# A two-layer encoder on one core: down's sum kept apart from the residual, the norm's factor of up moved behind it, and buffers placed anew

## The chip, the cores and the metric

The kernel runs on one core of a Trainium2 chip. The metric is the device time of one execution in microseconds (us), the median of several runs. The engines are called by the profile's names: PE is TensorE's matmul side and PEld its weight loads, DVE is VectorE, ACT is ScalarE, POOL is GpSimd, and SP is SyncE, whose queue issues all DMAs of this kernel.

## What is computed

A trunk of two layers over 1024 tokens of width 1024, in float32. Layer 0 mixes tokens by differential attention, layer 1 by neighbourhood attention on a grid. What follows the mixer is the same in both layers, and the change lies there:

```python
h = h + mix
h = h + swiglu(rmsnorm(h, norm_ffn[i]), ffn_w_gate[i], ffn_w_up[i], ffn_w_down[i])
gate = jax.nn.sigmoid(rmsnorm(h, norm_ple[i]) @ ple_w_gate[i])
h = h + gate * (p[i] @ ple_w_proj[i])
# swiglu(h, ...) = (silu(h @ w_gate) * (h @ w_up)) @ w_down, with 2816 hidden features
# rmsnorm(x, g) = x * rsqrt(mean(x * x) + eps) * g, per token
```

A norm over the last layer's output closes the trunk.

## The kernel before

Activations lie transposed: features on the 128 partitions, the 1024 tokens along the free dimension, in two halves f1 and f2 of 512. For precision every operand of a product is split in a high part (a cast, line 103 on ScalarE or 105 on GpSimd) and a low part (the difference, line 106 on VectorE), and every product is three matmuls (`PASSES`).

The feed-forward products use a Strassen scheme of seven products in place of eight. `blocks` (line 207) makes the seven weight operands from the raw weights: GpSimd forms the sums and differences (line 227), `split` casts them. `seven` (line 244) runs the products in the order 0, 5, 4, 1, 6, 3, 2 and calls `after` behind each, which takes an accumulator out of PSUM and combines it.

`out_proj` (line 634) adds the mixer's output to the residual x, writes x to memory (`hd`), and `moving_blocks` (line 146) makes the seven token operands `bt` from x times the norm's weights. It also adds up the squares of x (lines 672, 673). The norm's per-token factor, `rb`, is not applied there. `inverse_rms` forms it after the second product of the first group.

`gate_up` (line 677) has 11 pairs of hidden feature blocks. Each has a gate group and an up group of 84 matmuls (line 707). For gate, the sum is multiplied by `rb` (714), passed through silu (715), and multiplied by `rb` again on GpSimd (716), so that the up sum, multiplied in at line 718, needs no factor of its own. `hand_over` (746) makes down's seven operands of each pair, and they go to memory (`ad`), except the last pair's, which are kept.

`down` (line 790) goes over the pairs in five chunks (four of two pairs, one of three), and in each over four pairs of output blocks, `dp` and `dp + 4`. The operands come back from memory (`b`, line 787). Eight tiles `h` of 128 x 1024 are loaded from `hd` before (line 937), and every chunk's sums are added to them (line 828, some on VectorE from PSUM, some on GpSimd from a temporary).

`ple_proj` (line 853) and `ple` (883) end the layer: the norm (line 118) sums squares (123, 125), brings the factor to all partitions by two small matmuls (128, 136), and multiplies (139) into tiles `n`. The last norm's `n` go straight to the output (903).

Buffers: raw weights have two (`stage`), weight operands three slabs of 8 KB per partition and two more in the stage's own pool, and four buffers of 4 KB in `t4` hold temporaries, among them the weights' sums `s` and the products' `t`. Pools on the left are stacked in the order in which they are opened, so a pool that is opened after another was closed lies on the same memory, and a tile waits for the last access of the tile that lay there. In layer 0 the pool of x (four tiles of 8 KB, then 4 KB of sums of squares, 4 KB of squares and 8 KB of `n`) is followed on the same memory by the pools of the odd heads' q and k (24 KB), of v (24 KB) and of the even heads' q and k (24 KB).

The order of the instructions within each engine's queue is not the program's: a planner sets it at compile time, with a simulated timeline in which earlier program order goes first among what is ready. On the chip each queue is run in that order.

## Time and profile before

| | us |
|---|---|
| median of 3 runs | 3092.09 |
| lowest, highest | 3088.83, 3095.67 |
| the profiled execution's own time | 3095.93 |
| its span, first to last instruction | 3094.1 |

The page gives the busy time of each engine, the span in 40 slices, and the costliest groups of instructions. A group's row ends with the time that its engine sat idle ahead of it and what ended most of that. In a timeline a row has its start, its length, engine, line, operation, what it writes and reads, how many instructions were merged, and in brackets the idle time before it and what ended that. A wait for several things is put down to the one that came last.

### The profile page before, as it was taken

The numbers are of one execution on the slowest core, as the hardware profiler recorded it, in microseconds if no ns is written. First come the engines' busy times: TensorE is split into PE (matmuls) and PEld (weight loads), VectorE is DVE, ScalarE is ACT, GpSimd is POOL, SyncE is SP. The second block draws the span as 40 slices with busy tenths as digits, with TensorE's granted clock in tenths as the row PEclk, the third lists the DMA queues.
The fourth block names the chain that finished last, engine by engine and source line by source line (L and its number), as shares of the span: only waits on it lengthen the run. The fifth ranks groups of instructions, "written<-read, shape, count | busy, mean of one in ns | idle before, by whom it ended". The sixth has DMA issues, their size and how long they took to land. (4 is left out here: it accounts for less than half of the span.)

```text
span 3094.1 us, 38448 instructions
## 1 busy us (share of the span) xinstructions
PE 2820.4 (91%) x13272; PEld 2281.7 (74%) x13272; DVE 2277.1 (74%) x4023; ACT 1250.2 (40%) x2626; POOL 1572.7 (51%) x1408
## 2 busy tenths in 40 slices
PE   4999999997899999888899999999799999888888
PEld 4778778885677777666678888888577777666666
DVE  6697878787687787767576666666788877766666
ACT  3354546445343343222333544544434434322241
POOL 1234343435677777556422443333677777656522
PEclk8999999998899999999999999999899999999989
DMA  2101010324243333744232111135233333664222
GB/s 97 41 28 42 28 41 26 137 102 165 89 150 134 131 143 130 305 160 180 94 100 85 53 67 73 63 149 215 86 143 141 145 141 132 240 229 156 96 75 102
DMA packets 102291, 364.93 MB, mean 118 GB/s; under 512 B 11728, under 2 KB 13904, under 8 KB 98000
## 3 DMA queue, kind: packets, MB, share of 16 engines
q1 hardware_dynamic: 102096, 362.47, 32.2%
q8 instruction: 105, 1.72, 0.2%
q14 instruction: 90, 0.74, 0.1%
HBM read 249.18 MB, written 113.25 MB: 117 GB/s over the span
## 5 line engine op out<-in xcount | busy, mean ns | idle before, releaser
L707 PE MATMUL mm<-bt,w 128*128 128x512 f32 x3696 | 895.2, 404 | 51.0 <-ACT t L723 29.4
L707 PEld LDWEIGHTS mm<-bt,w 128*128 128x128 f32 x3696 | 707.3, 192 | 239.5 <-ACT t L723 38.5
L822 PE MATMUL mm<-b,w 128*128 128x512 f32 x1680 | 440.1, 416 | 76.8 <-ACT w L103 29.9
L106 DVE TENSOR_TENSOR w<-raw,w 128x512 fp32r<-128x512 f32 (+2 forms) x460 | 379.6, 845 | 129.3 <-ACT w L103 128.2
L822 PEld LDWEIGHTS mm<-b,w 128*128 128x128 f32 x1680 | 326.0, 198 | 184.9 <-ACT w L103 42.0
L103 ACT CAST w<-raw 128x512 fp32r<-128x512 f32 (+2 forms) x460 | 217.9, 498 | 479.3 <-DMA raw<-gu 170.3
L261 PE MATMUL d<-hnT,w 128*128 128x512 f32 x1536 | 386.2, 400 | 0.0
L261 PEld LDWEIGHTS d<-hnT,w 128*128 128x128 f32 x1536 | 287.2, 189 | 64.1
L105 POOL TENSOR_SCALAR w<-st 128x1024 fp32r<-128x1024 f32 (+3 forms) x128 | 146.5, 1146 | 360.3 <-PE mm L261 66.4
L828 POOL TENSOR_TENSOR h<-h,t 128x512 f32<-128x512 f32 x120 | 161.4, 1359 | 229.1 <-DVE t L828 196.3
L348 PE MATMUL d<-w,hnT 128*128 128x256 f32 x1536 | 227.8, 293 | 12.6 <-DVE v L106 7.8
L348 PEld LDWEIGHTS d<-w,hnT 128*128 128x128 f32 x1536 | 210.6, 196 | 23.6 <-DVE v L106 9.4
L106 DVE TENSOR_TENSOR w<-s,w 128x512 fp32r<-128x512 f32 (+2 forms) x184 | 194.8, 1064 | 26.4 <-ACT w L103 23.2
L106 DVE TENSOR_TENSOR w<-st,w 128x1024 fp32r<-128x1024 f32 (+3 forms) x128 | 142.6, 1118 | 91.6 <-POOL w L105 91.4
L421 ACT ACTIVATE e<-e,mx 128x1024 f32<-128x1024 f32 x128 | 147.4, 1152 | 133.7 <-DVE mx L419 125.8
L261 PE MATMUL mm<-hnT,w 128*128 128x512 f32 x768 | 189.3, 407 | 4.8 <-ACT hnT L103 3.3
L436 POOL TENSOR_SCALAR e<-e,rc 128x1024 f32<-128x1024 f32 x64 | 74.2, 1159 | 216.9 <-DVE rc L434 199.8
L261 PEld LDWEIGHTS mm<-hnT,w 128*128 128x128 f32 x768 | 147.7, 193 | 46.4 <-issue 8.3
L103 ACT CAST at<-tr 128x512 fp32r<-128x512 f32 (+2 forms) x288 | 131.8, 480 | 108.3 <-PE tr L571 69.5
L106 DVE TENSOR_TENSOR at<-tr,at 128x512 fp32r<-128x512 f32 (+2 forms) x288 | 155.8, 550 | 26.6 <-ACT at L103 19.9
L333 PE MATMUL s<-kh,qs 128*128 128x512 f32 (+2 forms) x384 | 154.1, 410 | 22.0 <-DVE mx L413 12.7
L567 POOL TENSOR_SCALAR e<-e,sm 128x384 f32<-128x384 f32 (+1 forms) x128 | 75.3, 590 | 184.3 <-DVE sm L566 158.3
(164 smaller groups left out, 5059.7 us busy)
## 6 DMA issues: line engine op xcount, KB each, us to landing
ad<-put SPq DMA_DIRECT2D x140, 512.0 KB, 2.7
b<-ad SPq DMA_DIRECT2D x140, 512.0 KB, 7.3
raw<-gu SPq DMA_DIRECT2D x88, 512.0 KB, 4.4
raw<-wd SPq DMA_DIRECT2D x40, 512.0 KB, 3.9
st<-wpg SPq DMA_DIRECT2D x32, 512.0 KB, 3.5
ot<-ot SPq DMA_DIRECT2D x14, 1024.0 KB, 3.9
o<-ot SPq DMA_DIRECT2D x14, 1024.0 KB, 8.4
st<-da_qk SPq DMA_DIRECT2D x16, 512.0 KB, 3.5
```

The costliest lines, as they stand in the source:

```text
L103: hi_engine.copy(out=w[0], in_=src)
L105: hi_engine.tensor_scalar(out=w[0], in0=src, scalar1=1.0, scalar2=0.0, op0=ALU.mult, op1=ALU.add)
L106: self.nc.vector.tensor_tensor(out=w[1], in0=src, in1=w[0].bitcast(F32), op=ALU.subtract)
L261: self.nc.tensor.matmul(ps, w[:, i, kt * P:(kt + 1) * P], self.hnT[half][:, j, kt, :], start=kt == 0 and n == 0, stop=kt == KT - 1 and n == 2)
L333: self.nc.tensor.matmul(s, qs[:, m, qc], (kh, kl)[part][:, m, kc], start=part == 0, stop=part == 1)
L348: self.nc.tensor.matmul(ps, self.hnT[t // 4][:, i, k, c], ws[k // 4][:, j, (k % 4) * 256:(k % 4 + 1) * 256], start=k == 0 and n == 0, stop ...
L421: nc.scalar.activation(out=e[m], in_=e[m], func=AF.Exp, bias=mx[:, m:m + 1], scale=SLOPES[h], accum_out=sm[:, m:m + 1])
L436: nc.gpsimd.tensor_scalar(out=e[0], in0=e[0], scalar1=rc[:, 0:1], scalar2=0.0, op0=ALU.mult, op1=ALU.add)
L567: nc.gpsimd.tensor_scalar(out=e[:, :n], in0=e[:, :n], scalar1=sm, scalar2=0.0, op0=ALU.mult, op1=ALU.add)
L707: self.end = nc.tensor.matmul(acc, w[b][:, i, k * P:(k + 1) * P], bt[b][:, j, k], start=first and k == 0 and n == 0, stop=k == 3 and n == ...
L822: nc.tensor.matmul(acc, w[b][:, i, q * P:(q + 1) * P], mv[b, q][:, j], start=first and q == 0 and m == 0, stop=q == n - 1 and m == 2, skip ...
L828: eng.tensor_tensor(out=o, in0=x, in1=y, op=ALU.add)
```

## The change

- `norm` has two `n` buffers in place of four. In `ple` the pool of the norm's tiles is opened on the right side.
- In `out_proj` the squares and the two differences of `moving_blocks` share one tag with two buffers in place of one buffer each.
- In layer 0's attention the pools are opened as odd, even, v.
- The weights' sums in `blocks` get a pool of their own with one buffer. In `down` the third temporary u3 is a half-size tile.
- `gate_up` no longer multiplies silu's output by `rb`. `rb` moves to a pool on the right that lives through `down`.
- `down` no longer loads the residual ahead. The first chunk writes its sums into `h` (copies by ScalarE where they were additions on VectorE). After the last chunk of each output pair the residual is loaded into `x`, `h` is multiplied by `rb` on GpSimd and x is added on VectorE.

```diff
 def norm
-            n = pool.tile([P, HALF], F32, tag="n", name="n", bufs=4)
+            n = pool.tile([P, HALF], F32, tag="n", name="n", bufs=2)
 def moving_blocks
-        t2 = pool.tile([P, HALF], F32, tag="t2", name="t2", bufs=1)
-        t3 = pool.tile([P, HALF], F32, tag="t3", name="t3", bufs=1)
+        t2 = pool.tile([P, HALF], F32, tag="t", name="t2", bufs=2)
+        t3 = pool.tile([P, HALF], F32, tag="t", name="t3", bufs=2)
 def out_proj
-                    sq = op.tile([P, HALF], F32, tag="sq", name="sq", bufs=1)
+                    sq = op.tile([P, HALF], F32, tag="t", name="sq", bufs=2)
 def blocks
-        sums = self.t4.tile([P, 2, HALF], F32, tag="t4", name="s")
+        sums = pool.tile([P, 2, room], F32, tag="s", name="s", bufs=1)
 def diff_attention
-            odd, vp, even = pool("da_qk1", 1), pool("da_v", 1), pool("da_qk0", 1)
+            odd, even, vp = pool("da_qk1", 1), pool("da_qk0", 1), pool("da_v", 1)
 def gate_up
-            pp, gp, sp, tp = pool("gput"), pool("ggt"), pool("gslab"), pool("gtmp")
+            ws, pp, gp, sp, tp = pool("gsum"), pool("gput"), pool("ggt"), pool("gslab"), pool("gtmp")
-            rb = tp.tile([P, S], F32, tag="rb", name="rb")
+            rb = self.rb
                         nc.scalar.activation(out=o, in_=o, func=AF.Silu)
-                        nc.gpsimd.tensor_tensor(out=o, in0=o, in1=rb[:, c], op=ALU.mult)
 def down
-                    w = self.blocks(parts, place)
+                    w = self.blocks(parts, place, sp, 3 * P)
+                    begin = chunk is CHUNKS[0]
...
                         elif b == 5:
-                            add(t["u2"], acc, t["p1"])
-                            add(lo[:, f2], lo[:, f2], t["u2"], nc.gpsimd)
+                            u2 = lo[:, f2] if begin else t["u2"]
+                            nc.vector.tensor_tensor(out=u2, in0=acc, in1=t["p1"], op=ALU.add)
+                            if not begin:
+                                gather(lo[:, f2], u2, nc.gpsimd)
                         elif b == 4:
-                            add(hi[:, f2], hi[:, f2], acc)
+                            if begin:
+                                nc.scalar.copy(out=hi[:, f2], in_=acc)
+                            else:
+                                gather(hi[:, f2], acc)
...
                         elif b == 6:
-                            add(t["u3"], acc, t["p1"])
-                            add(hi[:, f2], hi[:, f2], t["u3"], nc.gpsimd)
-                            add(hi[:, f1], hi[:, f1], t["u3"], nc.gpsimd)
+                            u3 = hi[:, f1] if begin else t["u3"]
+                            nc.vector.tensor_tensor(out=u3, in0=acc, in1=t["p1"], op=ALU.add)
+                            gather(hi[:, f2], u3, nc.gpsimd)
+                            if not begin:
+                                gather(hi[:, f1], u3, nc.gpsimd)
...
                     self.seven(banks, product, after)
+
+                    if chunk is CHUNKS[-1]:
+                        for dt in (dp, dp + 4):
+                            x = sp.tile([P, S], F32, tag="x", name="x", bufs=2)
+                            nc.sync.dma_start(out=x, in_=self.hd[dt])
+                            for c in (f1, f2):
+                                nc.gpsimd.tensor_tensor(out=h[dt][:, c], in0=h[dt][:, c], in1=self.rb[:, c], op=ALU.mult)
+                                nc.vector.tensor_tensor(out=h[dt][:, c], in0=h[dt][:, c], in1=x[:, c], op=ALU.add)
 def build
+                rp = tc.alloc_tile_pool(name=f"rb{layer}", bufs=1, side="right", reuse_waits="tile")
+                self.rb = rp.tile([P, S], F32, tag="rb", name="rb")
...
-                h = {t: hp.tile([P, S], F32, tag=f"h{t}", name=f"h{t}") for t in (0, 4, 1, 3, 7, 5, 2, 6)}
-                for dt in (0, 4, 1, 5, 2, 6, 3, 7):
-                    nc.sync.dma_start(out=h[dt], in_=self.hd[dt])
+                h = {t: hp.tile([P, S], F32, tag=f"h{t}", name=f"h{t}") for t in (0, 4, 1, 5, 3, 7, 2, 6)}
...
+                rp.release()
                 self.open_hn()
-                self.ple(layer, h, ps, pool("n"), proj)
+                np = tc.alloc_tile_pool(name=f"n{layer}", bufs=1, side="right", reuse_waits="tile")
+                self.ple(layer, h, ps, np, proj)
+                np.release()
```

## Rows read from the trace of the kernel before

**Rows 1.** The page, busy time of each engine and digits of the slices.

```profile
PE 2820.4 (91%) x13272; PEld 2281.7 (74%) x13272; DVE 2277.1 (74%) x4023; ACT 1250.2 (40%) x2626; POOL 1572.7 (51%) x1408
...
PE   4999999997899999888899999999799999888888
```

**Rows 2.** Groups by line: busy us, mean ns, idle before, its end.

```profile
L707 PE MATMUL mm<-bt,w 128*128 128x512 f32 x3696 | 895.2, 404 | 51.0 <-ACT t L723 29.4 <-DVE bt L106 10.4 <-DVE w L106 5.8
...
L822 PE MATMUL mm<-b,w 128*128 128x512 f32 x1680 | 440.1, 416 | 76.8 <-ACT w L103 29.9 <-ACT t L831 27.8 <-DMA b<-ad 11.9
...
L828 POOL TENSOR_TENSOR h<-h,t 128x512 f32<-128x512 f32 x120 | 161.4, 1359 | 229.1 <-DVE t L828 196.3 <-DMA h<-hd 29.1 <-ACT w L103 3.7
...
L716 POOL TENSOR_TENSOR gt<-gt,rb 128x512 f32<-128x512 f32 x88 | 129.9, 1495 | 25.6 <-ACT gt L715 25.6
...
L828 DVE TENSOR_TENSOR h<-h,mm 128x512 f32<-128x512 f32 x160 | 105.4, 678 | 45.6 <-POOL h L828 30.7 <-PE mm L822 11.6 <-DMA h<-hd 2.8
...
L106 DVE TENSOR_TENSOR v<-d,v 128x128 fp32r<-128x128 f32 x128 | 35.2, 284 | 31.6 <-ACT v L103 30.9
```

**Rows 3.** Timelines of the start: start, duration, operation, its wait and releaser.

```profile
59.18 1.42 DVE L106 TENSOR_TENSOR hnT<-n,hnT 128x256 fp32r<-128x256 f32 x4
...
61.01 1.48 ACT L103 CAST v<-d 128x128 fp32r<-128x128 f32 x8
...
62.45 13.69 PE L348 MATMUL d<-w,hnT 128*128 128x256 f32 x96 [7.78 <-DVE v L106]
75.97 22.64 PE L261 MATMUL d<-hnT,w 128*128 128x512 f32 x96
```

**Rows 4.** The tile of the sums, 1000 to 1240 us: groups by line.

```profile
L106 DVE TENSOR_TENSOR w<-s,w x24: 630/1561/1785, 1008.9 to 1231.5; 128x512 fp32r<-128x512 f32 x22, 128x256 fp32r<-128x256 f32 x2
...
L227 POOL TENSOR_TENSOR s<-s,raw x12: 745/1622/1630, 1006.8 to 1230.3; 128x512 f32<-128x512 f32 x11, 128x256 f32<-128x256 f32 x1
```

**Rows 5.** Timeline of one steady gate/up pair, layer 0.

```profile
1054.57 1.30 POOL L227 TENSOR_TENSOR raw<-raw,s 128x512 f32<-128x512 f32 x1 [1.30 <-DVE w L106]
...
1060.00 0.62 ACT L103 CAST w<-raw 128x512 fp32r<-128x512 f32 x1 [3.48 <-DMA raw<-gu]
...
1061.23 4.21 POOL L716 TENSOR_TENSOR gt<-gt,rb 128x512 f32<-128x512 f32 x3 [1.96 <-ACT gt L715]
...
1063.10 0.63 ACT L715 ACTIVATE gt<-gt 128x512 f32<-128x512 f32 x1 [1.42 <-DVE gt L714]
...
1064.25 39.61 PE L707 MATMUL mm<-bt,w 128*128 128x512 f32 x168 [2.16 <-ACT t L723]
...
1065.40 1.75 POOL L227 TENSOR_TENSOR s<-raw 128x512 f32<-128x512 f32 x1
```

**Rows 6.** Timelines of the begin of down, layer 0.

```profile
1257.21 9.28 SPq L937 DMA_DIRECT2D h<-hd  x8
...
1267.59 1.29 POOL L828 TENSOR_TENSOR h<-h,t 128x512 f32<-128x512 f32 x1 [14.99 <-DMA h<-hd]
...
1299.62 12.90 PE L822 MATMUL mm<-b,w 128*128 128x512 f32 x42 [3.63 <-ACT w L103]
```

**Rows 7.** Timeline of the last chunk of down, layer 0.

```profile
1482.37 2.71 POOL L828 TENSOR_TENSOR h<-h,t 128x512 f32<-128x512 f32 x2 [2.42 <-DVE t L828]
...
1486.43 2.13 PE L822 MATMUL mm<-b,w 128*128 128x512 f32 x8 [1.59 <-ACT w L103]
...
1495.41 1.29 POOL L828 TENSOR_TENSOR h<-h,t 128x512 f32<-128x512 f32 x1 [6.55 <-DVE t L828]
```

**Rows 8.** The same timeline, from the last output pair on.

```profile
1520.53 18.65 PE L878 MATMUL mm<-w 128*128 128x512 f32 x81 [1.44 <-POOL w L105]
...
1539.70 0.63 ACT L123 ACTIVATE acc<-h 128x512 f32<-128x512 f32 x1
```

**Rows 9.** Timeline of the end of the program.

```profile
3084.81 2.72 DVE L139 SCALAR_TENSOR_TENSOR n<-h,g,bc 128x512 f32<-128x512 f32 x4 [2.23 <-PE bc L136]
3087.70 2.81 DVE L139 SCALAR_TENSOR_TENSOR n<-h,g,bc 128x512 f32<-128x512 f32 x4 [0.17 <-DMA out<-n]
```

More of the change, by code (lines that the diff above doesn't have):

```diff
@@ L203, in packed, with blocks @@
         return place
-    def blocks(self, parts, place):
+    def blocks(self, parts, place, pool, room=HALF):
         nc = self.nc
@@ L694, in prepare @@
                     gates[pr] = gp.tile([P, 2, S], F32, tag="gt", name="gt", bufs=2)
-                return self.blocks([(raw[0][:, f1], raw[0][:, f2], raw[1][:, f1], raw[1][:, f2])], place)
+                return self.blocks([(raw[0][:, f1], raw[0][:, f2], raw[1][:, f1], raw[1][:, f2])], place, ws)
             def group(pr, which):
@@ L813, in down @@
                         parts.append((r[:, :, 0, 0], r[:, :, 1, 0], r[:, :, 0, 1], r[:, :, 1, 1]))
-                    w = self.blocks(parts, place)
+                    w = self.blocks(parts, place, sp, 3 * P)
                     banks = [ps.tile([P, HALF], F32, tag="mm", name="mm") for _ in range(4)]
-                    a2, b2 = (self.t4.tile([P, 2, HALF], F32, tag="t4", name="t") for _ in range(2))
-                    t = {"p1": a2[:, 0], "u2": a2[:, 1], "u3": b2[:, 0]}
+                    begin = chunk is CHUNKS[0]
+                    a2 = self.t4.tile([P, 2, HALF], F32, tag="t4", name="t")
+                    t = {"p1": a2[:, 0], "u2": a2[:, 1]}
+                    if not begin:
+                        t["u3"] = self.t4.tile([P, HALF], F32, tag="t4", name="t")
                     def product(b, acc, first):
@@ L824, in product, with gather @@
                                                  skip_group_check=True)
+                    lo, hi = h[dp], h[dp + 4]
+                    def gather(o, x, eng=nc.vector):
+                        eng.tensor_tensor(out=o, in0=o, in1=x, op=ALU.add)
                     def after(b, acc):
-                        def add(o, x, y, eng=nc.vector):
-                            eng.tensor_tensor(out=o, in0=x, in1=y, op=ALU.add)
-                        lo, hi = h[dp], h[dp + 4]
                         if b == 0:
@@ L837, in after @@
                         elif b == 1:
-                            add(lo[:, f1], lo[:, f1], acc)
+                            if begin:
+                                nc.scalar.copy(out=lo[:, f1], in_=acc)
+                            else:
+                                gather(lo[:, f1], acc)
                         elif b == 6:
-                            add(t["u3"], acc, t["p1"])
-                            add(hi[:, f2], hi[:, f2], t["u3"], nc.gpsimd)
-                            add(hi[:, f1], hi[:, f1], t["u3"], nc.gpsimd)
+                            u3 = hi[:, f1] if begin else t["u3"]
@@ L843, in after @@
+                            nc.vector.tensor_tensor(out=u3, in0=acc, in1=t["p1"], op=ALU.add)
+                            gather(hi[:, f2], u3, nc.gpsimd)
+                            if not begin:
+                                gather(hi[:, f1], u3, nc.gpsimd)
                         elif b == 3:
-                            add(hi[:, f1], hi[:, f1], acc)
+                            gather(hi[:, f1], acc)
                         elif b == 2:
-                            add(lo[:, f2], lo[:, f2], acc)
+                            gather(lo[:, f2], acc)
```

## The prediction

> **What bounds the kernel now.** I read the page first, for who is busy, then the groups by line, for what TensorE waits on, then the timelines of the four places that the change touches. On the page TensorE is busy 2820 us of 3094 and no other engine comes near it [rows 1]; its products are not changed. So the question is only which of its idle stretches go or come, and everything else counts as far as it ends one of them. The groups by line give those stretches in the two stages that are touched most: TensorE sat idle 51.0 us ahead of the gate/up products, 29.4 of them until the copy at L723, and 76.8 us ahead of down's products, 29.9 until a weight cast and 27.8 until the copy at L831 [rows 2]. Each total is for both layers. The copies are short; the reader is to see in the timelines what stands ahead of them in their queue. The first slice of the page, where TensorE is busy four tenths, is the third place.
>
> **The change part by part, each with its cost.**
>
> *Start.* The change swaps the pool of v with the pool of the even heads. By the pools' sizes in the code (x takes 32 KB, its squares and norms 16; q/k of the odd heads take 24 KB and v the next 24), v lies over the last quarter of x, the squares and n, so no v can be written before the last norm has read them. The timeline shows that: the first eight v casts run at 61.01, just behind the last hnT piece (59.18 + 1.42 = 60.6), though their products were long done, and TensorE, out of accumulators, idles 7.78 us and runs 96 value products from 62.45 to 75.97 [rows 3]. With v on free memory half of these, of the third quarter, can run while the fourth is normalised, and 48 x 13.69 / 96 = 6.8 us of work are left behind 60.6, partly overlapped with its last pieces. The end of the values moves from 76 to 64 at best: 12 us. Against this stand the v pieces on VectorE that now come before the last norm: 12 of 0.28 us [rows 2], 3.4 us on an engine that paces this stretch. I take -9, ends -4 and -12. Two n buffers in place of four make VectorE wait for a cast in the last quarter: +1, ends 0 and +3.
>
> *Moving blocks and first gate group.* Squares and the two differences share two buffers in place of three. Squares get double buffering, but a block's differences wait for the squares of the block before. TensorE's idle time ahead of the gate/up products outside the L723 wait is 51.0 - 29.4 = 21.6 us, 10.4 of it on these bt pieces [rows 2]. I take -2, ends -6 and +4, a modest share of either sign since both edits meet here.
>
> *Steady gate/up pairs.* The change drops 88 GpSimd products of 1.50 us, 130 us in all, from GpSimd's queue [rows 2]. What they hold up: in the pair shown, raw weights have landed by 1060.00, but the weights' first sum starts at 1065.40, straight behind three of these products (4.21 us from 1061.23). ScalarE waits 3.48 us for raw weights, which could only be loaded when the sums before had freed their buffer; then its queue holds the silu that waits on VectorE, and only then the copy that TensorE waits 2.16 us for [rows 5]. With sums some 4 us earlier the load, the cast and the copy come earlier by up to as much, more than the 2.16 us. TensorE's products set the bound: the gain cannot pass 29.4. Cover that goes: none, since silu's output is read later by VectorE and GpSimd, and a factor less only brings that forward. I take -20, nearer the upper end because the measured delay is twice the stall, ends 0 and -29. What is late next: the raw loads, behind two stage buffers.
>
> *Sums in a buffer of their own.* One buffer means that the next group's sum waits for the last reader of this one's: GpSimd's last subtraction of the up group ends at 1055.87, the next sum at 1065.40 is 9.5 us later [rows 5], so this wait is free. Four temporaries are left to the products' own tiles.
>
> *Begin of down.* Eight residual loads leave the SP queue, where they took 9.28 us of issue behind the b loads, and GpSimd no longer sits 14.99 us on them. Two GpSimd additions of 1.36 us per output pair go, 16 in all; two VectorE additions of 0.68 become ScalarE copies [rows 2, 6]. The queue freed here holds the weights' sums; in the trace TensorE's 3.63 us wait on a weight cast at 1299.62 follows [rows 6]. The b loads stay and with them TensorE's first waits. I take -5 for both layers, ends 0 and -9.
>
> *Middle of down.* Only the sums' buffer changes. GpSimd's order (product additions between the sums) stays in the code. I take -4, ends -20 (a third of the 57.7 us on casts and copies in [rows 2]) and +6, three stalls of 2 us if the compile-time order comes out worse.
>
> *End of down.* New: 16 GpSimd products by rb per layer, 32 in all, priced as the nearest row, L828's 1.36 us: 43.5 us; as many VectorE additions of 0.68; eight residual loads per layer on the SP queue, with two buffers, so a load waits for an addition and the next weight loads wait behind it. In a group of the last chunk GpSimd idles 2.42 and 6.55 us, more than 4 x 1.36 = 5.4, but a product of three of the four quarters is ready when the additions of 2.71 us end, and what comes next in that queue is the sum whose cast TensorE already waits 1.59 us for [rows 7]. The last pair's products meet the splits that TensorE waits 1.44 us for at L878; behind those the norm's squares wait in ScalarE's queue until 1539.70 anyway [rows 8]. Ends 0 (all in the idle 6.55) and +43.5 (all ahead of the sums). I take +14, a third: one and a third products of the four per pair.
>
> *Norms.* The very end: eight n in four buffers start at 3084.81, the fifth waits 0.17 for a landing at 3087.70 [rows 9], so a buffer turns round in 2.9 us. In two buffers four rounds follow each other: the starts are 84.8, 87.7, 90.6, 93.5, the last n ends at 94.9 in place of 90.5: +4, ends +3 and +5. The inner norms: +1, ends 0 and +3.
>
> The sum: -9 + 1 - 2 - 20 - 5 - 4 + 14 + 4 + 1 = **-20 us**. The profiled execution took 3095.93 (span 3094.1), 3.84 above the median of the runs shown; 3092.09 - 20 = **3072 us**.
>
> **A rule against it.** The VectorE difference that makes a weight's low part from two SBUF operands has a median of 1.56 us and reaches 1.79, while GpSimd's sums run beside it with a median of 1.62 [rows 4]; an addition with one operand in PSUM takes 0.68 [rows 2]. The Trainium skill, SBUF — State Buffer, section "Who interferes with whom", says why: a VectorE instruction with two SBUF inputs and a GpSimd instruction that reads SBUF exclude each other for a whole instruction. By that rule the new products by rb, beside new additions of two SBUF inputs, could each block one; by the row that is 1.56 - 0.68 = 0.9 us, 32 x 0.9 = 29 us more on VectorE, and the sum would be +9 if all of it reached TensorE. It gives back as much in gate/up, where 88 go.
>
> **Rivals.**
> - *More comes free* (0.21): the start at -12, gate/up at -29, the begin at -9, the middle at -20, the first group at -6, the end as taken with the norms: -12 - 29 - 9 - 20 - 6 + 20 = -56, 3036 us. For it: one GpSimd queue stands behind most of the stalls. Against: the raw loads and their two buffers stay.
> - *GpSimd's products were hidden* (0.13): then steady gate/up and middle give 0, the sum is +4, 3096 us. For it: the copy's wait ends on ScalarE behind a DMA, not on GpSimd directly.
> - *The products by rb go ahead of the weights' sums* (0.14), slower: the full 43.5 in the last chunk in place of 14, the sum is +9.5, 3102 us. It decides from 34 us on, 4.2 us per output pair. For it: they come before the next weights in program order, and are ready. Against: 6.55 us idle.
> - *The buffer does not free the sums, and the order made anew at compile time adds a stall per pair* (0.05): steady +29 in place of -20: +29, 3121 us. Against: 9.5 us of room.
>
> **How the numbers follow.** The forecast has 0.47, with 3050 to 3086 as its own range. Measurement can tell about 0.2%, 6.2 us. Faster: 0.47 + 0.21 = 0.68; within: 0.13; slower: 0.14 + 0.05 = 0.19. The range 3036 to 3102 leaves out the last rival and a third of the first and the third, whose prices are points with bounds on both sides: 0.05 + 0.07 + 0.05 = 0.17.
>
> **What would show it.** Right: v casts near 25 and values done near 66; L716 gone and GpSimd busy some 100 us less; the L723 wait below 10 us; no GpSimd wait on residual loads at the begin of down; the last n some 4 us later. Wrong: L723's wait unchanged, or TensorE's waits on weight casts in the last chunk above 4 us each.

## The result, and the profile after

The changed kernel takes 2965.18 us (median of 4 runs, 2963.36 to 2966.93) against 3093.88 of the kernel before in the same runs: a ratio of 0.9582, 95% interval 0.9561 to 0.9604. That is 129 us less, where 20 were forecast, and 71 us below the range's lower end. The direction was right and the size was not.

The page after, the rows that answer to [rows 1]:

```profile
PE 2768.3 (93%) x13272; PEld 2259.2 (76%) x13272; DVE 2255.2 (76%) x4039; ACT 1253.9 (42%) x2642; POOL 1451.2 (49%) x1336
...
PE   7999999997899999899799999999799999899987
```

TensorE is busy 52 us less for the same 13272 matmuls and idle 77 us less. The groups after, to be read against [rows 2] (down's products are on L824 now, the additions to h on L831):

```profile
L707 PE MATMUL mm<-bt,w 128*128 128x512 f32 x3696 | 886.5, 401 | 43.5 <-ACT bt L103 14.9 <-DVE bt L106 10.6 <-ACT t L722 10.6
...
L824 PE MATMUL mm<-b,w 128*128 128x512 f32 x1680 | 411.9, 401 | 34.3 <-ACT w L103 19.3 <-DVE t L838 9.6 <-DVE w L106 3.6
...
L831 POOL TENSOR_TENSOR h<-h,t 128x512 f32<-128x512 f32 x96 | 134.2, 1412 | 55.9 <-DVE t L853 41.9 <-DVE t L838 13.6
...
L831 DVE TENSOR_TENSOR h<-h,mm 128x512 f32<-128x512 f32 x144 | 95.3, 676 | 32.1 <-PE mm L824 22.4 <-POOL h L831 9.6
...
L869 POOL TENSOR_TENSOR h<-h,rb 128x512 f32<-128x512 f32 x32 | 46.1, 1447 | 10.1 <-DVE h L831 10.1
...
L870 DVE TENSOR_TENSOR h<-h,x 128x512 f32<-128x512 f32 x32 | 34.0, 1073 | 5.6 <-POOL h L869 5.6
```

Idle time ahead of gate/up's products went from 51.0 to 43.5 us, but ahead of down's from 76.8 to 34.3, and a down product lasts 401 ns in the mean where it lasted 416. The last two rows are the new work at the end of down.

Where the 129 us lie is worked out from the starts of TensorE's products in the two timelines, from the first product of a stage to the first of the next, both layers added:

| stretch | before | after | difference | forecast |
|---|---|---|---|---|
| start and attention, layer 0 | 710.3 | 690.9 | -19.4 | -9 +1 |
| out_proj and gate/up, to the last gate/up product | 1051.2 | 1018.8 | -32.5 | -2 -20 |
| from there to down's second chunk | 106.3 | 109.6 | +3.3 | -5 |
| second to fourth chunk | 306.7 | 236.2 | -70.6 | -4 |
| last chunk | 138.7 | 133.6 | -5.1 | +14 |
| ple_proj and ple | 273.6 | 269.5 | -4.2 | +1, with the next row |
| attention, layer 1 | 488.5 | 483.2 | -5.3 | |
| behind the last product | 18.9 | 23.4 | +4.5 | +4 |

More than half is the middle of down, the part that was thought least of. TensorE in that stretch of layer 0, and in the second 40 us of the program, as a table of windows (stretch, length, busy time and matmuls, granted clock, DMA share, GB/s), first the kernel before:

```profile
core 0: us, PE busy (x), PEclk, DMA share, GB/s
40.00:80.00 40.00, 20.65 (x125) 0.70 0.04 14
1293.00:1446.00 153.00, 131.20 (x506) 0.93 0.51 187
```

and after:

```profile
40.00:80.00 40.00, 37.69 (x205) 1.00 0.12 40
1258.00:1376.00 118.00, 118.00 (x505) 1.00 0.63 240
```

In the kernel before 153 us held 131.2 of busy time at a mean clock of 0.93 of full speed; after, the same products fill their 118 us without a gap at 1.00. So of the 35 us lost there, 21.8 were idle time and 13.2 were products that ran slowly. The row 40 to 80 answers the start: 37.7 us busy at clock 1.00, where the kernel before had 20.65 at 0.70.

The start itself, the timeline that answers to [rows 3]:

```profile
31.54 0.27 ACT L103 CAST v<-d 128x128 fp32r<-128x128 f32 x1 [0.17 <-PE d L348]
...
55.73 2.03 PE L261 MATMUL d<-hnT,w 128*128 128x512 f32 x8
57.60 4.47 PE L348 MATMUL d<-w,hnT 128*128 128x256 f32 x36
61.91 17.95 PE L261 MATMUL d<-hnT,w 128*128 128x512 f32 x76
```

The first v cast is at 31.5 in place of 61.0, from there on no wait ahead of the value products is longer than 0.8 us, their last run begins at 57.60, and products of the next stage are already done between them. And the end, the rows that answer to [rows 9]: n in pairs, each pair waiting 1.5 us for its buffers to be written out.

```profile
2951.69 1.41 DVE L139 SCALAR_TENSOR_TENSOR n<-h,g,bc 128x512 f32<-128x512 f32 x2 [2.23 <-PE bc L136]
...
2954.60 1.41 DVE L139 SCALAR_TENSOR_TENSOR n<-h,g,bc 128x512 f32<-128x512 f32 x2 [1.50 <-DMA out<-n]
2957.51 1.41 DVE L139 SCALAR_TENSOR_TENSOR n<-h,g,bc 128x512 f32<-128x512 f32 x2 [1.51 <-DMA out<-n]
2960.41 1.41 DVE L139 SCALAR_TENSOR_TENSOR n<-h,g,bc 128x512 f32<-128x512 f32 x2 [1.50 <-DMA out<-n]
```

### The profile page after: what moved, and what is told of

Same layout as the page of the kernel before. It is cut to its first block, busy times and chain, and to the rows that moved or that the text cites. A ratio compares the mean times of both kernels' runs of the same rounds, so it can differ in the third digit from the quotient of the medians.

```text
span 2964.9 us, 38407 instructions
## 1 busy us (share of the span) xinstructions
PE 2768.3 (93%) x13272; PEld 2259.2 (76%) x13272; DVE 2255.2 (76%) x4039; ACT 1253.9 (42%) x2642; POOL 1451.2 (49%) x1336
## 5 line engine op out<-in xcount | busy, mean ns | idle before, releaser
L707 PE MATMUL mm<-bt,w 128*128 128x512 f32 x3696 | 886.5, 401 | 43.5 <-ACT bt L103 14.9
L824 PE MATMUL mm<-b,w 128*128 128x512 f32 x1680 | 411.9, 401 | 34.3 <-ACT w L103 19.3
L824 PEld LDWEIGHTS mm<-b,w 128*128 128x128 f32 x1680 | 318.4, 190 | 119.1 <-ACT w L103 20.8
L106 DVE TENSOR_TENSOR w<-raw,w 128x512 fp32r<-128x512 f32 (+2 forms) x460 | 347.1, 782 | 70.7 <-ACT w L103 70.1
L105 POOL TENSOR_SCALAR w<-st 128x1024 fp32r<-128x1024 f32 (+3 forms) x128 | 134.8, 1054 | 317.9 <-PE mm L261 73.2
L106 DVE TENSOR_TENSOR w<-s,w 128x512 fp32r<-128x512 f32 (+2 forms) x184 | 174.0, 955 | 26.3 <-ACT w L103 24.5
L831 POOL TENSOR_TENSOR h<-h,t 128x512 f32<-128x512 f32 x96 | 134.2, 1412 | 55.9 <-DVE t L853 41.9
```

The costliest lines, as they stand in the source:

```text
L105: hi_engine.tensor_scalar(out=w[0], in0=src, scalar1=1.0, scalar2=0.0, op0=ALU.mult, op1=ALU.add)
L106: self.nc.vector.tensor_tensor(out=w[1], in0=src, in1=w[0].bitcast(F32), op=ALU.subtract)
L707: self.end = nc.tensor.matmul(acc, w[b][:, i, k * P:(k + 1) * P], bt[b][:, j, k], start=first and k == 0 and n == 0, stop=k == 3 and n == ...
L824: nc.tensor.matmul(acc, w[b][:, i, q * P:(q + 1) * P], mv[b, q][:, j], start=first and q == 0 and m == 0, stop=q == n - 1 and m == 2, skip ...
L831: eng.tensor_tensor(out=o, in0=o, in1=x, op=ALU.add)
```

## The experiments

"Shared temporaries" are the four buffers of `t4`. Chunk and pair lengths are those between the starts of TensorE's products; a mean pair is taken from the third pair's first product to the last product of the stage, over nine pairs. "More" and "less" without another name are against the kernel before in the same runs.

**What made down's weights late: three runs.** First the sums' own buffer alone, in down alone, on the kernel before:

```diff
-        sums = self.t4.tile([P, 2, HALF], F32, tag="t4", name="s")
+        sums = (self.t4.tile([P, 2, HALF], F32, tag="t4", name="s") if pool is None else
+                pool.tile([P, 2, room], F32, tag="s", name="s", bufs=1))
...
-                    w = self.blocks(parts, place)
+                    w = self.blocks(parts, place, sp, 3 * P)
```

Without a pool `blocks` takes the sums from `t4`; that is how the runs below switch between the two.

> The kernel before with one edit: the sums of down's weights get a buffer of their own; gate/up, the residual, the factor and the start stay. Theory A (in the shared temporaries a group's sums could only be made as late as the products' own temporaries let them, and every weight came just too late): TensorE's second to fourth chunk of down fall from 49 to 54 us to about 39.4 each, the whole run by 60 to 70 us, to 3025 to 3035. Rival B (the residual loads and additions at the begin of down made the weights late, and they never caught up): the chunks stay at 49 to 54 and the run at 3085 to 3100.

Measured 3009.16 us, ratio 0.9730 (0.9713 to 0.9748), 86 less. TensorE's group in down, and windows of its third and fourth part (second to fourth chunk, last chunk; columns as above):

```profile
L823 PE MATMUL mm<-b,w 128*128 128x512 f32 x1680 | 413.7, 401 | 30.1 <-ACT w L103 19.2 <-DVE w L106 4.1 <-DVE h L829 3.5
...
1302.00:1420.00 118.00, 117.69 (x503) 1.00 0.62 236
1420.00:1479.00 59.00, 59.00 (x253) 1.00 0.32 111
```

Second to fourth chunk took 39.9, 39.4 and 39.4 us, the last 59.0, in both layers. Theory A holds, and gives 16 us more than it asked for: it had left out the last chunk, which fell from 69 to 59. The residual's loads were still there and cost none of it; only the first chunk got longer (59.2).

The other way round, on the changed kernel:

```diff
-                    w = self.blocks(parts, place, sp, 3 * P)
+                    w = self.blocks(parts, place)
```

> The changed kernel with one edit: down's sums go back to the shared temporaries; gate/up keeps its own buffer and everything else stays. Theory A: down's chunks go back to 49 to 54 us, the run to 3025 to 3035. Rival B: the chunks stay at 39.4, the run within 10 us of 2965.

Measured 3059.14 us, ratio 0.9884 (0.9868 to 0.9899), 94 more than the changed kernel, where theory A had 60 to 70. The chunks were 45.7, 48.9, 48.8, 50.8 and 84.4 us in layer 0. In both layers together the second to fourth give 65 of the 94, as the theory had it, and the last, which it left out again, 33; the begin gives 10 back.

```profile
L825 PE MATMUL mm<-b,w 128*128 128x512 f32 x1680 | 439.9, 416 | 75.2 <-ACT t L836 28.3 <-ACT w L103 25.3 <-DMA b<-ad 11.4
```

75.2 us idle and 416 ns per product: the row of the kernel before, nearly to the digit. The last chunk shows what the products by `rb` cost when the sums are late too: 84 us in place of 69.

Is it the sums' new tile, or that they no longer share? The kernel before, with the sums left where they were and the products' temporaries moved out:

```diff
-                    a2, b2 = (self.t4.tile([P, 2, HALF], F32, tag="t4", name="t") for _ in range(2))
+                    a2 = sp.tile([P, 2, HALF], F32, tag="ta", name="t", bufs=2)
+                    b2 = sp.tile([P, HALF], F32, tag="tb", name="t", bufs=2)
```

> The kernel before with one edit: in down the products' temporaries (p1, u2, u3) get a pool of their own, with two buffers each, and the sums keep the four shared ones to themselves. Theory A, in the form that it is the sharing between sums and products' temporaries that made the weights late: second to fifth chunk at 39.4 and 59.0 us as with the sums moved out, the run at 2985 to 3010. Rival (it is something about the sums' new tile itself): chunks stay at 48 to 54 and 69, the run at 3085 to 3100.

Measured 3002.33 us, ratio 0.9705 (0.9686 to 0.9725). Chunks of 48.7, 42.7, 40.5, 40.3 and 59.0 in layer 0:

```profile
L823 PE MATMUL mm<-b,w 128*128 128x512 f32 x1680 | 414.6, 402 | 24.1 <-DMA b<-ad 9.2 <-DVE h L829 5.9 <-DVE t L829 5.1
...
1290.00:1414.00 124.00, 120.55 (x509) 1.00 0.65 246
1414.00:1473.00 59.00, 59.00 (x253) 1.00 0.29 103
```

So the cause lies in the ring of four buffers that both kinds take from; the sums' tile is not special. But both cures also add room, and no run gave a shared ring more than four buffers. That sharing alone is not enough to cost time is seen in the first chunk of the run before this one (the sums put back in the changed kernel). There sums and products share the four buffers as well, but a group takes two of them in place of three, and GpSimd has one addition per group in place of three: the last three groups take 9.8 us each, and GpSimd's differences end 4 to 8 us ahead of their group's first product. From the second group of the second chunk on, with three tiles per group, they end 6 to 8 us behind it (matched by count). Whether the third tile or the additions turn it was not tried. That the first chunk is no longer than before here (48.7), while it was 59.2 in the first run, is taken up below.

**The factor and gate/up: three runs.** The factor put back, on the changed kernel:

```diff
                         nc.scalar.activation(out=o, in_=o, func=AF.Silu)
+                        nc.gpsimd.tensor_tensor(out=o, in0=o, in1=rb[:, c], op=ALU.mult)
...
-                                nc.gpsimd.tensor_tensor(out=h[dt][:, c], in0=h[dt][:, c], in1=self.rb[:, c], op=ALU.mult)
```

> The changed kernel with GpSimd's product of gate by the norm's factor put back into gate/up, and the products by the factor at the end of down left out (the residual is still added there): the factor alone goes back. Theory C (GpSimd's 88 products held up the weights' sums): steady pairs go back from 39.4 to about 41.2 us, 20 x 1.8 = +36, less up to 8 for the products left out in down: 2990 to 3000. Rival D (the pairs became short through the sums' own buffer in gate/up): pairs stay at 39.4 to 39.8, the run at 2955 to 2970.

Measured 3010.6 us, 45 more than the changed kernel and 10 above the range expected. The product group of gate/up, and down's last chunk:

```profile
L707 PE MATMUL mm<-bt,w 128*128 128x512 f32 x3696 | 904.8, 405 | 86.6 <-ACT t L723 36.1 <-DVE t L725 24.6 <-ACT bt L103 15.0
...
1405.00:1464.00 59.00, 59.00 (x253) 1.00 0.43 150
```

From the third pair on, a pair took 42.4 us in place of 39.6; theory C had 41.2, the pair of the kernel before. The last chunk without the products by `rb` took 59.2 us, against 66.6 with them. Why 42.4 and not 41.2? The kernel before, with a sums' buffer of their own in gate/up alone:

```diff
-            pp, gp, sp, tp = pool("gput"), pool("ggt"), pool("gslab"), pool("gtmp")
+            ws, pp, gp, sp, tp = pool("gsum"), pool("gput"), pool("ggt"), pool("gslab"), pool("gtmp")
...
-                return self.blocks([...], place)
+                return self.blocks([...], place, ws)
```

> The kernel before with one edit: the sums of gate/up's weights get a buffer of their own; down keeps the shared temporaries, GpSimd's products by the factor stay. Theory C (one buffer for the sums costs in gate/up as long as GpSimd's products stand in the queue; with the factor put back the changed kernel's pairs took 42.6 us against 41.2 of the kernel before): pairs of 42.6, 20 x 1.4 = 28 us more, 3115 to 3125. Rival (the buffer costs nothing, the 42.6 have another cause): 3085 to 3100.

Measured 3119.93 us, ratio 1.0093 (1.0076 to 1.0110):

```profile
L708 PE MATMUL mm<-bt,w 128*128 128x512 f32 x3696 | 898.3, 403 | 80.6 <-ACT t L724 33.7 <-DVE t L726 23.5 <-DVE bt L106 10.3
```

And the changed kernel with gate/up's sums back in `t4`:

```diff
-                return self.blocks([...], place, ws)
+                return self.blocks([...], place)
```

> The changed kernel with one edit: gate/up's sums go back to the shared temporaries, down keeps its own buffer. Theory C (without the 88 products GpSimd has time enough, wherever the sums lie): pairs stay at 39.4 to 39.6, the run at 2960 to 2972. Rival (the own buffer carries part of gate/up's gain): pairs of 40 to 41.2, the run at 2980 to 3000.

Measured 2972.84 us, ratio 0.9612 (0.9597 to 0.9627).

```profile
L708 PE MATMUL mm<-bt,w 128*128 128x512 f32 x3696 | 886.8, 402 | 36.4 <-ACT t L723 19.3 <-ACT bt L103 11.6 <-DVE bt L106 3.8
```

The four cases side by side, mean pair from the third on in both layers: shared with GpSimd's products 41.1 us, own with them 42.3 and 42.4, own without 39.6, shared without 39.3. In gate/up the buffer helps nothing and costs 1.3 us per pair as long as the products are there. Removing them is the whole gain, 1.5 us per pair from the kernel before to the changed one. The run was 8 us longer than the changed kernel all the same, 5 of them in layer 1's first pairs by the profile, which puts it just above the 2972 of theory C.

**The start and the n buffers: two runs.** The swap of the pools alone, on the kernel before:

```diff
-            odd, vp, even = pool("da_qk1", 1), pool("da_v", 1), pool("da_qk0", 1)
+            odd, even, vp = pool("da_qk1", 1), pool("da_qk0", 1), pool("da_v", 1)
```

> The kernel before with the pool of v and the pool of the even heads swapped, n still in four buffers, nothing else. If the start of the changed kernel is due to this swap: 18 to 21 us less, near 3074, TensorE's granted clock from 40 to 80 us at 1.00 in place of 0.70. If my price for the idle time alone were right and the rest came from elsewhere: 9 us less, near 3085.

Measured 3077.56 us, ratio 0.9946 (0.9931 to 0.9961). That is 18 less, as the first theory had it, but not in the way that it had it: out_proj starts at 699.7 in the profile, 10.5 us earlier than before and 8.8 later than after, so the swap is about half of the start. Of the rest of the profile's gain 9 us lie in the second to fourth chunks of down, where nothing was edited. The window from 40 to 80 stands between the two kernels as well, and its clock does not reach the 1.00 expected:

```profile
40.00:80.00 40.00, 34.22 (x174) 0.87 0.11 36
```

Then the changed kernel with four n buffers:

```diff
-            n = pool.tile([P, HALF], F32, tag="n", name="n", bufs=2)
+            n = pool.tile([P, HALF], F32, tag="n", name="n", bufs=4)
```

> The changed kernel with one edit: four n buffers in every norm, as before. Theory G (two buffers cost only the tail, as in the prediction: +1, +1 and +4): the run falls by 4 to 6, to 2959 to 2961. Rival H (two buffers are what gave the second half of the start's gain and the 5 us of layer 1's attention): the start loses 8.5, layer 1's attention 5, the tail gains 5: about 2974, out_proj of layer 0 starting at 699 in place of 691.

Measured 2978.61 us, 13 more than the changed kernel: rival H, though it had 2974. In the profile the start is 5.0 us longer (out_proj at 695.9, not at 699), layer 1's attention 3.5, the tail 5.0 shorter. One profile can be off by a few us here, so all fourteen are compared: out_proj of layer 0 starts at 710.3 to 713.6 us in the five kernels without the swap, at 695.9 to 699.7 in the three with the swap and four buffers, and at 688.2 to 690.9 in the six with the swap and two. Between the means that is 13 us for the swap and 9 for the buffers. Layer 1's attention takes 486.0 to 489.2 us with four buffers and 483.2 to 486.5 with two, which overlap, so a gain there is not clear of the scatter. TensorE's small matmul by which a norm's factor is spread, up to 72 us, in the changed kernel:

```profile
L136 PE MATMUL bc<-diag,ones 128*128 128x256 f32 x8 | 3.5, 526 | 3.3 <-DVE diag L134 3.3
```

and with four buffers:

```profile
L136 PE MATMUL bc<-diag,ones 128*128 128x256 f32 x8 | 3.2, 491 | 7.6 <-DVE diag L134 7.6
```

With four buffers TensorE stood 7.6 us at these matmuls, with two 3.3. In the timelines of the two-buffer kernel value products stand ahead of three of the four groups of these matmuls in TensorE's queue; with four buffers they stand behind them. Its granted clock from 40 to 80 us falls back from 1.00 to 0.87.

**The moving blocks: one run.** On the kernel before:

```diff
-        t2 = pool.tile([P, HALF], F32, tag="t2", name="t2", bufs=1)
-        t3 = pool.tile([P, HALF], F32, tag="t3", name="t3", bufs=1)
+        t2 = pool.tile([P, HALF], F32, tag="t", name="t2", bufs=2)
+        t3 = pool.tile([P, HALF], F32, tag="t", name="t3", bufs=2)
...
-                    sq = op.tile([P, HALF], F32, tag="sq", name="sq", bufs=1)
+                    sq = op.tile([P, HALF], F32, tag="t", name="sq", bufs=2)
```

> The kernel before with one edit: the squares and the two differences of the moving blocks share two buffers under one tag. Theory I (this is what made out_proj 5.5 us shorter in each layer): out_proj of 37 in place of 42 us, the run at 3080 to 3084. Rival (out_proj became shorter because of what runs beside it): out_proj stays at 41 to 42.5, the run at 3088 to 3097.

Measured 3094.3 us, ratio 1.0012 (0.9998 to 1.0026): nothing. Groups from 700 to 868 us, the kernel before first:

```profile
L707 PE MATMUL mm<-bt,w 128*128 128x512 f32 x325 | 89.1, 438 | 14.8 <-DVE bt L106 5.4 <-ACT t L723 4.0 <-DVE w L106 3.7
L656 PE MATMUL mm<-o,w 128*128 128x512 f32 x96 | 28.8, 439 | 4.1 <-DVE w L106 3.7 <-DVE x L658 0.4
```

```profile
L707 PE MATMUL mm<-bt,w 128*128 128x512 f32 x335 | 88.6, 424 | 22.7 <-ACT t L723 12.3 <-ACT bt L103 5.8 <-ACT w L103 2.8
L656 PE MATMUL mm<-o,w 128*128 128x512 f32 x96 | 24.6, 394 | 2.5 <-DVE w L106 2.5
```

out_proj did fall to 36 and 37 us, as theory I had it, but the idle time ahead of gate/up's first products grew from 14.8 to 22.7. The gain is given back in the next stage.

**Down's first chunk, and a version that beats both: three runs.** In the first run above and after the change the first group of down took 22.6 us, with the sums in `t4` about 16. The new sums' tile lies on the memory of gate/up's last weights. Moved to other memory, and with four n buffers in every norm, on the changed kernel:

```diff
-            sp = st.enter_context(tc.tile_pool(name=f"dslab{layer}", bufs=1, reuse_waits="tile"))
+            sp, xp, ws = (st.enter_context(tc.tile_pool(name=f"{k}{layer}", bufs=1, reuse_waits="tile"))
+                          for k in ("dslab", "dx", "dsum"))
...
-            n = pool.tile([P, HALF], F32, tag="n", name="n", bufs=2)
+            n = pool.tile([P, HALF], F32, tag="n", name="n", bufs=4)
...
-                    w = self.blocks(parts, place, sp, 3 * P)
+                    w = self.blocks(parts, place, ws, 3 * P)
...
-                            x = sp.tile([P, S], F32, tag="x", name="x", bufs=2)
+                            x = xp.tile([P, S], F32, tag="x", name="x", bufs=2)
```

> The changed kernel with two edits: down's sums lie on memory that gate/up's last weights do not use, and the embedding norms have four n buffers again. Theory E (the first sums of down had to wait for the memory of gate/up's last weights): the first chunk falls from 54.5 to about 46 us in both layers, 2 x 8 = -16, and the tail behind the last product from 23.4 to 19 us, -4.5: 2942 to 2948. Rival F (GpSimd's handing over of the last up tile comes first anyway): the first chunk stays at 54 and only the tail falls: 2960.

Measured 2973.8 us, which neither had: the four n buffers cost more at the start than the tail gave (the run with four n buffers alone, above, shows that), so two edits in one kernel hid each other. The first chunk fell by 2 to 3 us only, to 51.6 and 52.4.

```profile
1209.57 0.74 POOL L227 TENSOR_TENSOR s<-raw 128x256 f32<-128x256 f32 x1
...
1227.02 0.68 DVE L839 TENSOR_TENSOR h<-mm,t 128x512 f32<-128x512 f32 x1
...
1227.75 1.65 PE L825 MATMUL mm<-b,w 128*128 128x512 f32 x3 [5.20 <-DVE h L839]
```

The first sum now starts 1.6 us ahead of gate/up's last product, where in the changed kernel it starts 9.0 behind it, but then TensorE waits 5.2 us for an addition in VectorE's queue. Better, on the changed kernel:

```diff
-                    w = self.blocks(parts, place, sp, 3 * P)
+                    w = self.blocks(parts, place, None if chunk is CHUNKS[0] else sp, 3 * P)
...
-            n = pool.tile([P, HALF], F32, tag="n", name="n", bufs=2)
+            n = pool.tile([P, HALF], F32, tag="n", name="n", bufs=2) if i < 3 * DEPTH else pool.tile(
+                [P, HALF], F32, tag="nf", name="n", bufs=4)
```

> The changed kernel with two edits: in down's first chunk alone the sums lie in the shared temporaries (free there, and not on memory of gate/up), and the last norm alone has four n buffers. If the lateness of the first sums is what makes the first chunk 54.5 us long: from gate/up's end to the second chunk 49.6 in place of 54.8 in each layer, -10, and -5 in the tail: 2948 to 2953. If the first group waits for the handing over all the same: only the tail, 2960.

Measured 2951.98 us (2950.25 to 2953.92), ratio 0.9550 (0.9531 to 0.9568), as expected. From gate/up's end to the second chunk it took 49.6 and 49.4 us, and the wait on the weight cast, 19.3 us in the changed kernel, is no longer among the three longest of down's group:

```profile
L826 PE MATMUL mm<-b,w 128*128 128x512 f32 x1680 | 412.9, 401 | 24.2 <-DVE t L840 11.3 <-DMA b<-ad 10.2 <-DVE h L833 1.0
```

The changed kernel ran beside other runs of the kernel before; its times (2963.36 to 2966.93) and these do not overlap, its ratio's interval (from 0.9561) and this one's (up to 0.9568) just do. Last, on this kernel:

```diff
-                    if chunk is CHUNKS[-1]:
-                        for dt in (dp, dp + 4):
+                    todo = [dp - 1] if chunk is CHUNKS[-1] and dp else []
+                    if chunk is CHUNKS[-1] and dp == KT // 2 - 1:
+                        todo.append(dp)
+                    for e in todo:
+                        for dt in (e, e + 4):
```

> The kernel of the run before (first sums in the shared temporaries, four n buffers in the last norm) with one edit: in down's last chunk the products by the factor and the residual's additions of an output pair are issued one pair later, behind the next pair's products; those of the last pair stay where they are. Theory J (what costs the last chunk 7.6 us per layer is the place of these products in GpSimd's and VectorE's queues, ahead of the next weights): the chunk falls from 66.9 to 60 to 63 us, the run by 8 to 14, to 2938 to 2944. Rival K (it is their sheer amount on the two engines): the chunk stays above 65, the run at 2948 to 2956.

Measured 2951.19 us, ratio 0.9544 (0.9528 to 0.9560), with last chunks of 68.1 and 67.3: the outcome of rival K. But the run tests neither J nor K: in layer 0's last chunk GpSimd's instructions stand in the same order as in the run before it, since the order is made anew at compile time, so the products were not moved at all. Whether their place or their amount costs the 7.6 us stays open.

## Why the prediction was right in direction and wrong in size

**Sums in a buffer of their own, "so this wait is free", and the middle of down, "only the sums' buffer changes", -4 with ends of -20 and +6.** This step failed: it measured -70.6, and -86 for the whole run when done alone. It was judged in gate/up, where the buffer gains nothing (and beside GpSimd's products is not free either: 1.3 us per pair), and carried over to down. A group of either stage takes three tiles in turn from the four buffers, one for the sums and two for the products, but down's groups are half as long (42 matmuls, 9.8 us). What I did not read is how far ahead of their use the sums are made. In the kernel before, GpSimd and SyncE in the third chunk (timeline), and the landing time of the load shown (from the DMA view of 1342 to 1343 us):

```profile
1342.51 0.38 SPq L810 DMA_DIRECT2D raw<-wd  x1
...
1360.53 1.28 POOL L828 TENSOR_TENSOR h<-h,t 128x512 f32<-128x512 f32 x1 [7.15 <-DVE t L828]
1361.77 0.74 POOL L227 TENSOR_TENSOR s<-raw 128x256 f32<-128x256 f32 x1
...
raw<-wd SPq DMA_DIRECT2D x1, 512.0 KB, 6.9
```

By count the tenth load of down's weights belongs to the tenth sum. It was issued at 1342.51 and landed 6.9 us later, near 1349. The sum started at 1361.77, 19 us after the issue, straight behind an addition for which GpSimd had stood idle 7.15 us. That addition takes what TensorE had just finished. So every group's weights waited for the products of the group ahead, and TensorE for these weights: the stage went round in a loop, 49 to 54 us per chunk in place of 39.4. After:

```profile
1344.22 0.75 POOL L227 TENSOR_TENSOR s<-raw 128x256 f32<-128x256 f32 x1 [0.81 <-DMA raw<-wd]
1344.41 0.33 SPq L809 DMA_DIRECT2D raw<-wd  x1
```

This sum starts when its load has landed. Over the third and fourth chunk it is 13 to 19 us from a load's issue to its sum in the kernel before and 7 to 11 after; GpSimd's last difference of a group ends 6 to 8 us behind the group's first product before, and 13 to 15 us ahead of it after (matched by count). That the shared ring of four brings this about is shown by the three runs; that it does so by the queue order made at compile time is read from the trace, not tried by itself.

The bound was wrong as well: "a third of the 57.7 us" of idle time. The slow products that follow such stops belong to the price. In the third and fourth chunk of the kernel before, after three of the stops, of 1.9, 2.5 and 3.2 us, a run of products started 0.43 us apart in place of 0.234, and the stretch had a granted clock of 0.93, a mean of the levels 1.2 and 2.4 GHz.

**End of down, +14.** This term was right: with the sums in place, the products by `rb` cost 66.6 - 59.2 and 66.9 - 59.0, 15.3 us together. The end fell by 5.1 all the same, since the sums' buffer gave 20 there.

**Begin of down, -5.** Wrong in sign, +3.3. The missing loads did free GpSimd, but the new tile for the sums lay on memory that gate/up still used, and I did not look up where it lies. In the kernel before the first sum of down starts 10 us ahead of gate/up's last product (at 1239.48):

```profile
1229.51 0.73 POOL L227 TENSOR_TENSOR s<-raw 128x256 f32<-128x256 f32 x1
```

After, it starts 9 us behind that product (at 1203.41), and TensorE waits for its weights:

```profile
1212.43 1.17 POOL L227 TENSOR_TENSOR s<-raw 128x256 f32<-128x256 f32 x1
...
1215.22 6.05 PE L824 MATMUL mm<-b,w 128*128 128x512 f32 x18 [9.69 <-ACT w L103]
```

With the first chunk's sums in `t4` the two layers go from 53.5 to 49.6 and from 52.7 to 49.4, -7.2, between the -5 and the -9 of the text.

**Steady gate/up pairs, -20 with ends of 0 and -29.** Right: from the third pair on -13.3 and -14.1, 27 us. The waits on the copy fell from 29.4 to 10.6 us, a little above the 10 that the text named as a sign of being right.

**Moving blocks and first group, -2.** Within its ends: what is left of the -32.5 is -5.1, and alone the edit is worth nothing.

**Start, -9 and +1.** The swap was priced about right: -10.5 in the profile of the run that has nothing else, -13 between the means of the kernels, with an end of -12. The mechanism was that of the text, but it counted idle time alone, and the granted clock rose as well (0.70 to 0.87 from 40 to 80 us). The n buffers were priced wrong: two in place of four gave another 9 us there, 5 by the run that puts them back, in place of costing 1. I priced a buffer count as waiting time only; in the timelines it also changes which products TensorE's queue holds ahead of a norm's matmul. That this order is the reason was not tried by itself: with two buffers the pool of x also ends 4 KB earlier.

**The tail, +4.** It was +4.5, by the mechanism of the text: four rounds of two.

**The rule against it.** The new additions of two SBUF operands took 1073 ns in the mean where those with one operand in PSUM took 676. That is 0.40 us more for each of 32, 13 us on VectorE, not 29. In the rest of the kernel it went the other way. The differences that make the weights' low parts, in the changed kernel and then in the run with the 88 GpSimd products put back:

```profile
L106 DVE TENSOR_TENSOR w<-raw,w 128x512 fp32r<-128x512 f32 (+2 forms) x460 | 347.1, 782 | 70.7 <-ACT w L103 70.1
...
L106 DVE TENSOR_TENSOR w<-s,w 128x512 fp32r<-128x512 f32 (+2 forms) x184 | 174.0, 955 | 26.3 <-ACT w L103 24.5
```

```profile
L106 DVE TENSOR_TENSOR w<-raw,w 128x256 fp32r<-128x256 f32 (+1 forms) x460 | 370.1, 834 | 65.3 <-ACT w L103 64.5
...
L106 DVE TENSOR_TENSOR w<-s,w 128x512 fp32r<-128x512 f32 (+2 forms) x184 | 183.1, 1014 | 50.3 <-ACT w L103 49.4
```

Both groups together take 521 us without those products and 553 with them, 32 us. The Trainium skill, SBUF — State Buffer, section "Who interferes with whom", has VectorE instructions with two SBUF inputs and GpSimd's SBUF reads exclude each other; the traces agree in direction in both places.

**The rivals.** None of them held for the change as a whole. "More comes free" came nearest and stopped at -56, because it too held the middle of down at -20. The products by `rb` did go ahead of the weights' sums in part, at the price forecast; they decided nothing beside the rest. The stall per pair of the last rival did appear, with its +29, but only in the run that gives gate/up's sums their own buffer and keeps the 88 products.

## What to carry to other kernels

When temporaries of two kinds share one ring of buffers, measure for each group how far ahead of its use the operand is made: from the landing of its load to the instruction that reads it, and from its end to the product that needs it. Here the lead was negative in every group from the second to the fourth chunk, and breaking the loop gave back nearly all idle time of that stretch and its slow products, not the share that the longest wait has. A change to a buffer that is worth nothing in one stage says nothing of another with shorter groups.

## What the runs showed that I had not expected

Fewer buffers can be faster: two n tiles gave 13 us over four, and the order of TensorE's queue had changed with them. And one buffer for the sums was slower in gate/up by 29 us while GpSimd had its 88 products, and 86 us faster in down. A shared ring, put back in the changed kernel, cost nothing from the second group of down on while a group took two of its four buffers, and 65 us in the next three chunks of the two layers, where it took three.
